# A streaming encoder layer on one core: 27 paired slots with all of conv a, weights summed by DMA, scan state kept in PSUM, branch A's norm moved into single slots

## The chip, the cores and the metric

The kernel is written for one Trainium2 chip and uses one of its cores. The metric is the device time of one execution in microseconds (us). The core has the engines TensorE (PE; the page shows its weight loads apart, as PEld), VectorE (DVE), ScalarE (ACT), GpSimd (POOL) and SyncE (SP), each with a queue of its own that it works off in order. Nearly all transfers are issued by SyncE; its queue and those of the other engines wait on semaphores. The program is written in Python with a tile library: pools hand out SBUF tiles by a tag with a fixed number of buffers, and a write into a tile waits until the last reader of the tile before it is done. PSUM has eight banks of 2 KB per partition.

## The reference

One layer over 1024 prompt rows and 32 sample rows (1056 columns in the kernel, which keeps channels on the partitions), with two branches from one input projection:

```python
proj = x @ w_in + b_in
a_val, a_glu, a_gate, z, xbc, dt_raw, g_a, g_b, g_p = jnp.split(proj, idx, axis=-1)

u = a_val * jax.nn.sigmoid(a_glu)
u, new_buf_a = causal_dwconv(u, buf_a, conv_a_w, conv_a_b)          # 31 taps
u = jax.nn.silu(layer_norm(u, norm_a_g, norm_a_b)) * jax.nn.silu(a_gate)
out_a = u @ w_a_out

xbc, new_buf_b = causal_dwconv(xbc, buf_b, conv_b_w, conv_b_b)      # 4 taps
xs, Bm, Cm = jnp.split(jax.nn.silu(xbc), [...], axis=-1)
dt = jax.nn.softplus(dt_raw + dt_bias)
y, h_new = ssd_scan(xs_h, dt, A, Bm, Cm, h0)       # chunks of 64 in the reference
y = (y + d_skip * xs_h).reshape(bsz, L, D_INNER)
out_b = gated_rmsnorm(y, z, gnorm_w) @ w_b_out

merged = sigmoid(g_a) * out_a + sigmoid(g_b) * out_b
x_new = layer_norm(ALPHA * x + merged @ w_out + sigmoid(g_p) * (p @ w_ple), ln_g, ln_b)
```

D_MODEL is 1024, the scan has 32 heads of 64 in 4 groups with a state of 128. In a scan chunk, with decays E and dec: y = (diagonal part) + E * (C times the carried state h), and h becomes dec * h + S, where S comes from the chunk's own B and x.

## The kernel before, in words

**Precision.** An fp32 product is made of three matmuls on parts of fewer bits: weights and activations are split into `hi` and `lo` (hi by ACT, lo = value - hi by DVE), and `three` (L191 ff.) issues hi*lo, lo*hi and hi*hi. So each 128-column tile of weights costs PE three passes and costs ACT and DVE a split.

**The stages in order.** The *start* loads x and p, splits weights (`wq_split`) and activations (`x_split`, `x_sum`, `t_split`), computes the embedding product p @ w_ple (`ple_group`, L569; eight tiles whose results are stored to `d_ple`) and dt (`dt_products`, `dt1`). Then come 24 *pair slots* P0 to P23 (`pair_slot`, L815): each makes two tiles of 128 projection columns with seven products of half size instead of eight (operands `OPND` with names like n2, t3, t4; weights r11, r12, r21, r22 and their sums), 168 matmuls of 264 columns in banks B0, B1, C and A. 40 *single slots* C0 to C39 follow (`slot`, L288): one tile each, 72 matmuls of 352 columns in three groups. B0 to B15 multiply by w_b_out, A0 to A7 by w_a_out, and W0 on by w_out with the last norm.

**The order of the work.** Each slot has named stages: loads first (`ld0`, the weights of slot s + 2, `ld`), stores (`st`), `d0`, the split of the next slot's weights, `a0`, `d1`, then the matmul groups with `a1` after the first third and `pm`, `a2` after the second, then `d2`, the fill, `pe` and `end`. `at(slot, stage, fn)` puts a piece of work into a stage; nothing else orders it, so what is written earlier stands earlier in each engine's queue. The fill (`run_fill`, L246) takes taps of conv a (31 DVE operations per half tile, `cae_u` and `cao_u`) until the DVE time that the program has counted for the slot reaches 11.0 us, or 14.2 us in a single slot with a scan chunk (in a pair: 2.82 us per position).

**Conv a and conv b.** Conv a needs pairs of tiles glu and val: five of the eight are made in pairs, tiles 5, 6 and 7 in single slots. Conv b (B, C and xs tiles) has three DVE taps per tile (`cb_t`) in the slot after it.

**Weights of a pair.** `pw_load` (L480) loads four quarters of 256 KB, `pw_sum` (L496) adds quarters on DVE into the tile `sx` or in place, and `pw_hi`, `pw_lo` split the seven results; `prep_act` and `prep_dve` (L503, L510) say at which of the seven positions of a pair this is done for the next.

**The scan.** `ssd_group` (L945) runs the 9 chunks (128 columns) of a group, one per single slot. In a chunk's first slot PE transposes (`pe_a`, at the end); in its second slot DVE and ACT prepare M, X and B2 (`prep`, stage `a0`), E is loaded, and PE makes `yd`, `yo` and S at the slot's end (`pe_d`, first in stage `pe`); in the third slot's `d0` DVE combines them (`update`, L1029): yo * E, + yd, four steps into the xs tiles, hT * dec, + S. The groups begin at C1, C10, C21 and C31.

**Branch A's norm.** Conv a's results are stored to `d_ca`. From C34 on (S_OB - 6 and later) they are loaded again, four at a time, summed (`ln_sum`), the sum over partitions is made on PE (`bcast_pe`, L328: three matmuls with ones onto all 128 rows) and broadcast through a row in memory (`ln_away`, `ln_back`); then the tiles are loaded again, centred and squared in B1 to B4, the reciprocal root follows (`rstd_chain`, L351), and `u_scale`, `u_act`, `u_mul` and the splits make w_a_out's operand. z tiles (`z_tile`, L1109) stay in SBUF until the scan of their group is done. Tiles for all of this are recycled in order by `tget` and `tput` (unit T), and smaller ones by U.

Of the kernel before, what the change touches and what calls it, by code (L numbers as in the profile page):

```python
# [60 lines left out]
def pair_tiles():  # L61

    gate = lambda n: ("gate", n, GATE_OFF[n // 8] + 128 * (n % 8))
    G = lambda n: (gate(n), gate(n + 1))
    C = lambda t: (("glu", t, O_GLU + 128 * t), ("val", t, O_VAL + 128 * t))
    X = lambda n: ("xs", n, O_X + 128 * n)
    return [G(0), G(2), C(0), G(8), G(4), G(10), G(6), C(1), G(12), G(16), G(14), C(2), G(18), G(20), G(22), G(24),
            C(3), G(26), G(28), G(30), C(4), (("B", 0, O_B), ("C", 0, O_C)), (X(0), X(1)), (X(2), X(3))]


def slot_tiles():
# [58 lines left out]
def emit(nc, tc, I, O, ctx):  # L130
# [197 lines left out]
    def bcast_pe(src, bks):  # L328

        out = []  # L330
        for (c0, c1), b in zip(GR, bks):
            ps = psum(b)
            mm(ps[:, :GN], ones, src[:, c0:c1])
            out.append(ps)
        return out

    def bcast_copy(pss, dst, scale=1.0):
        for (c0, c1), ps in zip(GR, pss):
            act(dst[:, c0:c1], ps[:, :GN], AF.Copy, scale=scale)
# [1446 lines left out]
```

## Time and profile before

| what | value |
|---|---|
| median of 3 runs | 1592.32 us (1592.23 to 1593.13) |
| the profiled execution | 1592.68 us, its span 1591.0 us |
| mean granted TensorE clock | 0.984 |
| busy: PE, DVE, ACT, POOL | 1527.2, 1296.9, 808.6, 3.0 us |
| start (up to P0) | 49.39 us |
| P0 to P23 | 49.39 to 558.78 |
| C0 to C39 | 558.78 to 1185.64 |
| B0 to B15 | 1185.64 to 1386.73 |
| A0 to A7, then W0 to the end | 1386.73 to 1481.12, then to 1591.0 |

How to read the lines below: a line of the timeline gives the start in us, the length in us, engine, line of the program, operation, output<-inputs, shapes and how many are put together. A line of the waits gives the waiting engine, what it makes and at which line, `<-` the engine and tile waited for, then the sum of the idle us, how many times, and the longest. A line of the groups ends with busy us, mean ns of one, and idle us before them. A line of the windows gives a stretch of the span, its length, the busy time of each engine with its instructions, the granted clock (PEclk), the DMA engines' share and GB/s. DMA lines give KB and the us from issue to landing.

### The profile page before, as it was taken

The numbers are of one execution on the slowest core, as the hardware profiler recorded it, in microseconds if no ns is written. First come the engines' busy times: TensorE is split into PE (matmuls) and PEld (weight loads), VectorE is DVE, ScalarE is ACT, GpSimd is POOL, SyncE is SP. The second block draws the span as 40 slices with busy tenths as digits, with TensorE's granted clock in tenths as the row PEclk, the third lists the DMA queues.
The fourth block names the chain that finished last, engine by engine and source line by source line (L and its number), as shares of the span: only waits on it lengthen the run. The fifth ranks groups of instructions, "written<-read, shape, count | busy, mean of one in ns | idle before, by whom it ended". The sixth has DMA issues, their size and how long they took to land.

```text
span 1591.0 us, 26642 instructions
## 1 busy us (share of the span) xinstructions
PE 1527.2 (96%) x10823; PEld 1481.8 (93%) x10823; DVE 1296.9 (82%) x1763; ACT 808.6 (51%) x1391; POOL 3.0 (0%) x14
## 2 busy tenths in 40 slices
PE   7899999999999989999999999999798999999997
PEld 6899999999999989999999999999688999999997
DVE  6888899999898599988988889888666887676654
ACT  6654334433434556666675666576564543333333
POOL 0000000000000000000000000000000000000000
PEclk9999999999999999999999999999899999999998
DMA  7252444442231134424252542336636171587422
GB/s 254 108 203 98 155 136 137 136 157 103 87 116 55 55 101 89 112 69 123 77 120 66 110 106 63 88 106 187 187 136 240 61 249 57 199 331 257 144 87 78
DMA packets 134377, 208.43 MB, mean 131 GB/s; under 512 B 28071, under 2 KB 84391, under 8 KB 134254
## 3 DMA queue, kind: packets, MB, share of 16 engines
q1 hardware_dynamic: 134254, 206.72, 41.9%
q8 instruction: 85, 1.39, 0.4%
q14 instruction: 38, 0.31, 0.1%
HBM read 156.49 MB, written 50.19 MB: 130 GB/s over the span
## 4 chain that ended last, share of the span: by engine, by line
PE 76%; DVE 12%; DMA 5%; ACT 4%; issue 2%; SPq 0%; DVEq 0%; ACTq 0%
PE ps L192 75%; DMA d_base<-cb_t 1%; PE ps L992 1%; DVE cao_u L176 1%; DVE cae_u L176 1%; DMA d_yn<-cbo_t 1%; DMA L_t<-d_accp 1%; DMA cat_t<-d_ca 1%; DVE sx L172 1%; DVE cb_t L176 0%; DVE wlo L172 0%; DMA d_gate<-ga_t 0%; DVE dt_u L176 0%; DVE acc_t L172 0%; DVE cb_u L176 0%
## 5 line engine op out<-in xcount | busy, mean ns | idle before, releaser
L176 DVE SCALAR_TENSOR_TENSOR cae_u<-uin_u,par,cae_u 128x1086 f32<-128x1086 f32 x120 | 161.3, 1344 | 0.0
L176 DVE SCALAR_TENSOR_TENSOR cao_u<-uin_u,par,cao_u 128x1086 f32<-128x1086 f32 x112 | 150.5, 1344 | 0.0
L186 ACT ACTIVATE whi<-wraw 128x1024 fp32r<-128x1024 f32 x65 | 68.5, 1054 | 67.5 <-PE ps L192 42.8
L186 ACT ACT_TABLE_LOAD x77 | 98.8, 1283 | 7.1 <-DMA out_conv_b<-vin_t 4.9
L172 DVE TENSOR_TENSOR wlo<-wraw,whi 128x1024 fp32r<-128x1024 f32 x65 | 79.3, 1219 | 24.6 <-ACT whi L186 24.5
L186 ACT ACTIVATE vin_t<-ps,par 128x352 f32<-128x352 f32 (+5 forms) x88 | 39.1, 476 | 107.3 <-PE ps L192 107.3
L186 ACT ACTIVATE L_t<-L_t,tk 128x128 f32<-128x128 f32 (+1 forms) x272 | 80.4, 381 | 0.0
L176 DVE SCALAR_TENSOR_TENSOR cb_t<-vin_t,par,cb_t 128x1059 f32<-128x1059 f32 x60 | 79.1, 1319 | 1.2
L186 ACT ACTIVATE zt_t<-ps,par 128x352 f32<-128x352 f32 x48 | 26.4, 554 | 75.3 <-PE ps L192 75.0
L172 DVE TENSOR_TENSOR acc_t<-acc_t,ps 128x352 f32<-128x352 f32 x72 | 36.6, 518 | 33.1 <-PE ps L192 33.0
L186 ACT ACTIVATE gb_t<-ps,par 128x528 f32<-128x528 f32 x26 | 18.2, 701 | 88.7 <-PE ps L192 74.8
L172 DVE TENSOR_TENSOR M<-ps,E 128x512 f32<-128x512 f32 (+1 forms) x32 | 20.4, 637 | 49.0 <-PE ps L192 45.3
L192 PE MATMUL ps<-n2l,w_2h 128*128 128x264 f32 x192 | 55.5, 289 | 3.7 <-ACT ga_t L186 3.7
L192 PE MATMUL ps<-t3l,w_4h 128*128 128x264 f32 x192 | 54.6, 284 | 2.3 <-ACT ga_t L186 2.3
L192 PE MATMUL ps<-n2h,w_2l 128*128 128x264 f32 x192 | 55.2, 288 | 0.0
L192 PE MATMUL ps<-n2h,w_2h 128*128 128x264 f32 x192 | 55.1, 287 | 0.0
L192 PE MATMUL ps<-t4l,w_6h 128*128 128x264 f32 x192 | 54.6, 285 | 0.3 <-ACT gb_t L186 0.3
L192 PE MATMUL ps<-t3h,w_4l 128*128 128x264 f32 x192 | 54.5, 284 | 0.0
L192 PE MATMUL ps<-t4h,w_6h 128*128 128x264 f32 x192 | 54.4, 284 | 0.0
L192 PE MATMUL ps<-t4h,w_6l 128*128 128x264 f32 x192 | 54.4, 283 | 0.0
L192 PE MATMUL ps<-t3h,w_4h 128*128 128x264 f32 x192 | 54.3, 283 | 0.0
L192 PE MATMUL ps<-x0l_t,whi 128*128 128x352 f32 x117 | 41.9, 358 | 8.9 <-ACT sg_t L186 5.0
(878 smaller groups left out, 5910.4 us busy)
## 6 DMA issues: line engine op xcount, KB each, us to landing
r<-in_w SPq DMA_DIRECT2D x96, 256.0 KB, 3.1
wraw<-in_w SPq DMA_DIRECT2D x39, 512.0 KB, 4.3
L_t<-d_accp SPq DMA_DIRECT2D x30, 512.0 KB, 6.5
d_yn<-cbo_t SPq DMA_DIRECT2D x16, 528.0 KB, 3.6
wraw<-in_wb SPq DMA_DIRECT2D x16, 512.0 KB, 3.6
yraw_t<-d_yn SPq DMA_DIRECT2D x15, 528.0 KB, 7.7
gs_t<-d_gate SPq DMA_DIRECT2D x15, 528.0 KB, 5.9
E<-d_expa SPq DMA_DIRECT2D x56, 128.0 KB, 4.7
```

Of the source, the lines that this page charges most:

```text
L172: nc.vector.tensor_tensor(out, a, b, op)
L176: nc.vector.scalar_tensor_tensor(out, a, s, b, op0, op1)
L186: nc.scalar.activation(out, a, f, **kw)
L192: nc.tensor.matmul(out, l, r, start=start, stop=stop, skip_group_check=more)
L992: nc.tensor.transpose(pX[:nt, j * P:(j + 1) * P], XS[j][:, sl], ident)
```

## The change

Six things are changed together.

1. **27 pairs, 34 singles.** The glu and val tiles 5 to 7 go into three more pairs; a conv a pair stands in every third place of the table instead of more widely apart.

```diff
-    return [G(0), G(2), C(0), G(8), G(4), G(10), G(6), C(1), G(12), G(16), G(14), C(2), G(18), G(20), G(22), G(24),
+    return [G(0), G(2), C(0), G(8), G(4), C(1), G(10), G(6), C(2), G(12), G(16), C(3), G(14), G(18), C(4), G(20), G(22), C(5),
...
-    return ca(5) + bcx(1) + z(0) + ca(6) + bcx(2) + z(1)[:2] + ca(7) + bcx(3) + z(1)[2:] + z(2) + z(3)
+    return bcx(1) + z(0) + bcx(2) + z(1) + bcx(3) + z(2) + z(3)
...
-    SSD0 = [S_CL + i for i in (1, 10, 21, 31)]
+    SSD0 = [S_CL + i for i in (1, 10, 19, 28)]
```

2. **Weights of a pair.** `pw_sum` is gone. The sums s1, s3 and s2 are made in memory transfers: SyncE loads the first summand and GpSimd issues DMAs that add the others onto it, one for s1 and s3 and two for s2; r12, the third that s2 takes, is added later (`pw_s4`). That is six loads by SyncE (four before) and five DMAs by GpSimd (none before).

```diff
+    PARTS = {"r11": ("11",), "r12": ("12",), "r22": ("22",), "s1": ("21", "22"), "s3": ("21", "11"), "s2": ("11", "21", "22")}
...
     def pw_load(i, n):
         if i < len(PAIRS):
-            t = raw_tile(n, f"{n}_{i}")
-            load(t, I["w1"][2 * i + (n[1] == "2"), :, 512 * (n[2] == "2"):512 * (n[2] == "2") + 512])
-            pr[i, n] = t
+            t = pr[i, n] = raw_tile(n, f"{n}_{i}")
+            load(t, pw_src(i, PARTS[n][0]))
+            for q in PARTS[n][1:]:
+                nc.gpsimd.dma_start(t, pw_src(i, q), accum_op=ALU.add)
+
+    def pw_s4(i):
+
+        if i < len(PAIRS):
+            nc.gpsimd.dma_start(pr[i, "s2"], pw_src(i, "12"), accum_op=ALU.add)
```

On DVE, in a pair (names w_1l to w_4l are lo halves of the seven weights, r and s the quarters and sums, ga, gb and sg results, cae and cao taps), the order before is:

```order
L172 TENSOR_TENSOR w_1l<-sx_2595,w_1h 128x512
L172 TENSOR_TENSOR sx_2595<-r_9_2421,r_9_2423 128x512
L172 TENSOR_TENSOR ga_t_2555<-ga_t_2555,ps_2663 128x528
L172 TENSOR_TENSOR gb_t_2556<-gb_t_2556 128x528
L172 TENSOR_TENSOR w_2l<-sx_2595,w_2h 128x512
L172 TENSOR_TENSOR w_3l<-r_9_2522,w_3h 128x512
L172 TENSOR_TENSOR sx_2595<-r_9_2522,sx_2595 128x512
L172 TENSOR_TENSOR ga_t_2555<-ga_t_2555,ps_2597 128x528
L172 TENSOR_TENSOR w_4l<-r_9_2421,w_4h 128x512
```

The same place after the change, still on DVE:

```order
L171 TENSOR_TENSOR w_1l<-s_9_2505,w_1h 128x512
L175 SCALAR_TENSOR_TENSOR cae_u_2324<-uin_u_1867,par,cae_u_2324 128x1086
L175 SCALAR_TENSOR_TENSOR cao_u_2356<-uin_u_1867,par,cao_u_2356 128x1086
L171 TENSOR_TENSOR sg_t_2605<-sg_t_2605,ps_2720 128x528
L171 TENSOR_TENSOR w_2l<-s_9_2441,w_2h 128x512
L175 SCALAR_TENSOR_TENSOR cae_u_2324<-uin_u_1867,par,cae_u_2324 128x1086
```

The two sums into sx are gone, and taps of conv a stand between the splits.

3. **The start.** `wq_split(2)` and `(3)` stand in the work list ahead of the sums T3 and N2, the embedding's results 0 to 5 and 7 go to tiles of xpool (tags n2l, t3l, t3h) instead of U, `dt1` goes into the work list, and P0's weights come by `pw_load` as in 2.

4. **The scan.** The matmuls of the carried part (`pe_o`) go to stage `pm`, after two thirds of the slot; DVE's `carry` (stage `d2`) writes hT * dec into the bank of S and multiplies y by E in PSUM; `pe_d` adds onto both banks; `update` is a copy of S by ACT and the four steps into xs.

```diff
-                yd, S = psum(5), psum(7)
+                y, S = d["y"], d["S"]
...
-                    mm(yd[64 * u:64 * u + 64, j * P:j * P + nt], X[:nt, 64 * h:64 * h + 64], d["L3"][:, h, :])
...
-                mm(S, B2[:nt, :], M[:nt, :512])
...
+                    mm(y[64 * u:64 * u + 64, j * P:j * P + nt], X[:nt, 64 * h:64 * h + 64], d["L3"][:, h, :],
+                       i == 0 and j == 0, True, True)
+                mm(S, B2[:nt, :], M[:nt, :512], i == 0, True, True)
...
+            def pe_o(i=i, sl=sl, nt=nt):
+
+                d = st[i]
+                d["y"], d["S"] = psum(6), psum(7)
+                if i:
+                    for j in range(4):
+                        mm(d["y"][:, j * P:j * P + nt], hcols(i)[:, j * P:(j + 1) * P], Ct_[0][:, sl], j == 0, True, True)
+
+            def carry(i=i, nt=nt):
+                if i:
+                    d = st[i]
+                    h3 = hcols(i).rearrange("p (h c) -> p h c", h=8)
+                    tt(d["S"][:, :].rearrange("p (h c) -> p h c", h=8), h3,
+                       decb[:, 8 * g:8 * g + 8, i].unsqueeze(2).to_broadcast([P, 8, 64]), ALU.mult)
+                    y3 = v4(d["y"][:, :])[:, :, :nt]
+                    tt(y3, y3, v4(d["E"][:, :4 * nt]), ALU.mult)
...
+                act(hc, S)
...
+            at(s0 + i + 1, "pm", pe_o)
+            at(s0 + i + 1, "d2", carry)
```

On PE, at the end of a slot with a chunk (cbo tiles are xs, B and C after conv b, hT the state, L the decays, x7 the last operand of the slot's matmuls), before:

```order
L192 MATMUL ps_7176<-x7h_t_118,whi_6944 128x352
L192 MATMUL ps_7208<-L_t_6927,X_3_7106 64x128 x8
L192 MATMUL ps_7218<-cbo_t_6158,hT_t_6505 128x128 x4
L192 MATMUL ps_7209<-M_3_7105,B_3_7107 128x512
L992 MATMUL ps_7224<-ident,cbo_t_6401 128x128
```

After, first at two thirds of such a slot, then at its end:

```order
L191 MATMUL ps_8033<-x7h_t_117,whi_7837 128x352
L191 MATMUL ps_8059<-cbo_t_7040,hT_t_7392 128x128 x4
L191 MATMUL ps_8074<-x0l_t_104,whi_7837 128x352
...
L191 MATMUL ps_8074<-x7h_t_117,whi_7837 128x352
L191 MATMUL ps_8059<-L_t_7823,X_3_7998 64x128 x8
L191 MATMUL ps_8060<-M_3_7997,B_3_7999 128x512
L966 MATMUL ps_8120<-ident,cbo_t_7287 128x128
```

The four matmuls on hT have moved ahead of the last third, and the eight on L now add onto the same tile (ps_8059) that DVE multiplies between the two. On DVE the slot after, with `update` and `prep`, reads before:

```order
L172 TENSOR_TENSOR M_4_7259<-ps_7374,E_4_7239 128x512
L172 TENSOR_TENSOR M_4_7259<-M_4_7259,ps_7364 128x512
L176 SCALAR_TENSOR_TENSOR cbo_t_6401<-cbo_t_6401,par,M_4_7259 128x128
...
L172 TENSOR_TENSOR hT_t_6505<-hT_t_6505,decb 128x512
L172 TENSOR_TENSOR hT_t_6505<-hT_t_6505,ps_7365 128x512
L172 TENSOR_TENSOR wlo_7412<-wraw_7237,whi_7410 128x1024
L172 TENSOR_TENSOR M_5_7417<-ps_7380,tk 128x512
```

After, from the last step into xs to the first tap of conv b (the two rows that write ps are `carry`):

```order
L175 SCALAR_TENSOR_TENSOR cbo_t_7402<-cbo_t_7402,par,ps_8059 128x128
L171 TENSOR_TENSOR wlo_8147<-wraw_7978,whi_8145 128x1024
L171 TENSOR_TENSOR M_4_8152<-ps_8120,tk 128x512
L171 TENSOR_TENSOR X_4_8153<-ps_8120,tk 128x512
L171 TENSOR_TENSOR M_4_8152<-ps_8121,mask 128x128
L171 TENSOR_TENSOR L_t_7976<-L_t_7976,M_4_8152 128x1024
L171 TENSOR_TENSOR ps_8215<-hT_t_7392,decb 128x512
L171 TENSOR_TENSOR ps_8214<-ps_8214,E_4_8133 128x512
L175 SCALAR_TENSOR_TENSOR cb_t_8160<-vin_t_7973,par,cb_t_8160 128x1059
```

The four operations of 512 columns at the slot's head are gone, and two stand behind `prep`, ahead of the taps.

5. **Branch A's norm.** Its base A0 is S_OB - 17, in the single slots: the sums in C17 and C18, the mean's matmuls after C18, and from C21 to C28 one tile per slot is loaded, centred, squared and stored again (`ca_away`); the u steps go one tile per slot from B6 on. A z tile that is made more than four slots ahead of its use is stored to `d_z` and loaded again (five tiles).

```diff
-        at(B + t // 4 * 2, "ld", ca_load, t)
-        at(B + 1 + t // 4 * 2, "d1", ln_center, t)
...
+    A0 = B - 17
...
+        c = A0 + 4 + t
+        at(c - 1, "ld", ca_load, t)
+        at(c, "d1", ln_center, t)
+        at(c, "a1", ln_square, t)
+        at(c + 1, "st", ca_away, t)
```

6. **Sums over partitions.** `rows_pe` takes the place of `bcast_pe` and of the sums in hi and lo parts: three matmuls with 32 columns of ones into three groups of 32 partitions of one bank.

```diff
+    def rows_pe(src):
+
+        ps = psum(5)
+        for g, (c0, c1) in enumerate(GR):
+            mm(ps[32 * g:32 * g + 32, :GN], ones[:, :32], src[:, c0:c1])
+        return ps
```

More of the change, by code (lines that the diff above doesn't have):

```diff
@@ L206, in emit @@
     nc.gpsimd.memset(ones, 1.0)
-    nc.gpsimd.memset(ones_r[:, :].bitcast(F32), 1.0)
     nc.gpsimd.memset(epsb, EPS)
@@ L225, in emit @@
     d_yn = dpool.tile([16, P, NT], F32, name="d_yn")
+    d_z = dpool.tile([16, P, NT], F32, name="d_z")
     d_ca = dpool.tile([8, P, NT], F32, name="d_ca")
@@ L325, in slot, with rows_copy @@
         run(s, "end")
[L328 to L339, printed above, removed]
+    def rows_pe(src):
[3 more added lines that the diff above has]
+        return ps
+    def rows_copy(ps, dst, scale=1.0):
+        for g, (c0, c1) in enumerate(GR):
+            act(dst[0:1, c0:c1], ps[32 * g:32 * g + 1, :GN], AF.Copy, scale=scale)
     def newton(r, m, t):
@@ L461, in emit @@
     r_quad(0, 1)
-    w0 = xpool.tile([P, 8, H], F32, tag="t3l", name="w0", bufs=1)
+    w0 = ppw.tile([P, 8, H], F32, tag="o0h", name="w0", bufs=1)
     wdt = xpool.tile([P, 1024], F32R, tag="t3h", name="wdt", bufs=1)
@@ L575, in ple_group @@
             three(ps[:, :GN], wh[:, w], wl[:, w], ph[:, k, c0:c1], pl_[:, k, c0:c1], k == 0, k == 1)
-        if g == 0 and m in (4, 6):
-            both = xpool.tile([P, 2, NT], F32, tag=f"t3{'hl'[m // 2 - 2]}", name=f"pl{m}", bufs=1)
+        if g == 0 and m in (0, 2, 4, 7):
+            both = xpool.tile([P, 2, NT], F32, tag={0: "n2l", 2: "t3l", 4: "t3h", 7: "t3l"}[m], name=f"pl{m}", bufs=1)
             pls[m], pls[m + 1] = both[:, 0, :], both[:, 1, :]
-        if g == 0 and m < 4:
+        if g == 0 and m == 6:
             pls[m] = U.get([P, NT], F32, "pl")
@@ L743, in step @@
             f(*a)
-    for n in ("r11", "r21", "r22", "r12"):
+    for n in ("r11", "s1", "s2", "r12", "s3"):
         pw_load(0, n)
@@ L753, in emit @@
     xs2 = lambda n: [(x_sum, n, q) for q in range(2)]
-    work.extend(xs4("B11") + xs4("B12") + xs2("D1") + [(wdt_split,)] + xs4("B21") + xs4("B22") + xs2("T3") + xs2("N2"))
+    ts2 = lambda n, q: [(t_split, n, q, i) for i in range(2)]
+    work.extend(xs4("B11") + xs4("B12") + xs2("D1") + [(wdt_split,)] + xs4("B21") + xs4("B22") + [(wq_split, 2), (wq_split, 3)])
     for m in range(4):
@@ L781, in emit @@
     x_put((1, 1))
-    for n in ("r21", "r22"):
-        pw_load(1, n)
     pw_hi(0, 3, "r12")
     pw_lo(0, 3, "r12")
+    pw_load(1, "r12")
     for q in range(2):
@@ L1109, in z_tile, with away, back @@
     def z_tile(g, j, zt, s):
-        q = {}
+        q = {"z": zt}
+        def away():
+            load(d_z[4 * g + j], zt)
+            tput(zt)
+        def back():
+            q["z"] = tget(name="zt")
+            load(q["z"], d_z[4 * g + j])
+        if s - cur[0] > 4:
+            at(cur[0] + 1, "st", away)
+            at(s - 1, "ld", back)
         def gate():
             x = XSs[4 * g + j]
-            tt(x, x, zt, ALU.mult)
+            tt(x, x, q["z"], ALU.mult)
         def square():
-            act(zt, XSs[4 * g + j], AF.Square)
+            act(q["z"], XSs[4 * g + j], AF.Square)
         def add():
             if j == 0:
-                zst[g] = zt
+                zst[g] = q["z"]
             else:
-                tt(zst[g], zst[g], zt, ALU.add)
-                tput(zt)
+                tt(zst[g], zst[g], q["z"], ALU.add)
+                tput(q["z"])
         at(s, "d1", gate)
```

163 lines of the change are left out of this document (60 added, 103 removed).

## The prediction, made before the changed kernel was run

> **What bounds the kernel now.** I read the page first, then the busy time by stage, then who TensorE (PE) waits for, stage by stage. The page:
>
> ```profile
> span 1591.0 us, 26642 instructions
> ...
> PE 1527.2 (96%) x10823; PEld 1481.8 (93%) x10823; DVE 1296.9 (82%) x1763; ACT 808.6 (51%) x1391; POOL 3.0 (0%) x14
> ...
> PEclk9999999999999999999999999999899999999998
> ...
> PE 76%; DVE 12%; DMA 5%; ACT 4%; issue 2%; SPq 0%; DVEq 0%; ACTq 0%
> ```
>
> PE is busy for 96% and most of the chain that ended last is PE. So two things can shorten the run: less PE work, and fewer stretches in which PE waits or runs at half clock. The table by stage says where those are (its rows are: the start; P0 to P6; P7 to P22; P23 to C1; C2 to C35; C36 to B3):
>
> ```profile
> core 0: us, PE busy (x) PEld busy (x) DVE busy (x) ACT busy (x) POOL busy (x), PEclk, DMA share, GB/s
> 0.00:49.39 49.39, 36.99 (x193) 35.45 (x193) 34.74 (x55) 33.14 (x69) 1.93 (x12) 0.93 0.63 232
> 49.39:206.40 157.01, 147.11 (x1186) 145.63 (x1186) 135.58 (x182) 73.92 (x130) 1.09 (x2) 0.99 0.39 136
> 206.40:533.07 326.67, 326.67 (x2691) 326.67 (x2689) 294.28 (x374) 130.44 (x222) 0.00 (x0) 1.00 0.34 115
> 533.07:591.08 58.01, 49.49 (x327) 48.33 (x326) 44.79 (x52) 33.77 (x56) 0.00 (x0) 0.94 0.32 88
> 591.08:1105.36 514.28, 513.70 (x3455) 483.35 (x3453) 456.07 (x609) 332.44 (x608) 0.00 (x0) 0.99 0.40 98
> 1105.36:1245.58 140.22, 121.23 (x750) 112.71 (x748) 98.03 (x127) 75.11 (x125) 0.00 (x0) 0.94 0.54 179
> ```
>
> ```profile
> 908.07:1000.39 92.32, 92.32 (x633) 86.80 (x632) 80.97 (x114) 58.91 (x112) 0.00 (x0) 1.00 0.33 79
> 1386.73:1467.84 81.11, 81.11 (x507) 81.11 (x505) 59.24 (x83) 31.14 (x41) 0.00 (x0) 1.00 0.82 296
> 728.70:732.10 3.40, 3.40 (x14) 3.40 (x14) 3.37 (x8) 1.03 (x2) 0.00 (x0) 0.50 0.42 90
> ```
>
> Undisturbed stretches give PE's price of each kind of slot: P7 to P22 is 326.67 / 16 = 20.42 us per pair; C23 to C28, each with one scan chunk, 92.32 / 6 = 15.39 us; A0 to A6, plain single slots, 81.11 / 7 = 11.59 us. A chunk therefore costs 3.80 us. What a stage took beyond these prices is loss. P0 to P6 took 157.01 against 7 x 20.42 + 0.9 (nine transposes) = 143.8: 13.2 lost. The start has 49.39 - 36.99 = 12.4 idle and about 3.5 at 0.93 of the clock: 16 lost. P23 to C1 lost about 12 (8.5 idle, the rest clock). C36 to B3 is 4 x 15.39 + 14.49 + 3 x 11.59 and some 2.7 of sums over partitions, 113.6; it took 140.22: 26.6 lost. PE's waits name the culprits:
>
> ```profile
> PE ps L192 <- ACT acc_t L186: 6.9, 4, 4.4
> PE ps L192 <- DVE M L172: 6.9, 1, 6.9
> PE ps L192 <- ACT ga_t L186: 6.0, 2, 3.7
> PE ps L192 <- DVE t4l L172: 5.8, 2, 5.4
> PE ps L192 <- ACT sg_t L186: 5.0, 1, 5.0
> PE ps L192 <- ACT zt_t L186: 4.8, 2, 3.9
> PE ps L192 <- DVE wq2l L172: 4.4, 1, 4.4
> PE ps L192 <- DVE vin_t L172: 3.5, 1, 3.5
> ```
>
> **Pairs for singles.** Six single slots (conv a tiles 5 to 7) become three pairs: 6 x 11.59 - 3 x 20.42 = 69.54 - 61.26 = 8.3 us less PE work. It is on the path, since PE never idles in either undisturbed stretch.
>
> **Weights summed by DMA.** This takes four DVE additions out of each pair and puts five GpSimd DMAs and two SyncE loads in.
>
> ```profile
> L172 DVE TENSOR_TENSOR sx<-r,r 128x512 f32<-128x512 f32 x48 | 33.2, 692 | 1.7
> ...
> r<-in_w SPq DMA_DIRECT2D x96, 256.0 KB, 3.1
> ```
>
> 4 x 0.69 = 2.8 us per pair leave DVE. From P7 on that brings PE nothing: DVE already has 20.42 - 294.28 / 16 = 2.0 us to spare per pair, and the fill puts conv a taps of the three added tiles in the room. It does shorten DVE's queue in P0 to P2, before the fill. The added traffic is 7 x 256 KB per 20.42 us, 90 GB/s on top of 115; by the stage's share of 0.34 that makes about 0.6, so I let it hide. No trace shows a DMA that adds: the nearest row is the plain load, 3.1 us to landing. The tightest of the five is the fourth summand of s2: its issue follows position 4 (14.6 us into the pair) and ScalarE (ACT) wants it at position 0 of the next pair (23.3), so 8.7 us for one landing; I take cost 0 and treat a slow one as a rival. The Trainium skill ("DMA: Bandwidth & Descriptors", section "Anatomy of one DMA — SWDGE (gpsimd) path") gives about 2.0 us and the bytes at 436 GB/s for a GpSimd DMA, which would be an estimated 2.6 us here and would leave the sum as it is; no run here shows one yet.
>
> **The start.** Weight splits 2 and 3 now stand ahead of the sums T3 and N2, the embedding's results go to xpool tiles instead of recycled units, and the last sum for P0 no longer stands in ACT's queue.
>
> ```profile
> ACT pl_u L186 <- PE ps L192: 6.0, 1, 6.0
> DVE x7l_t L172 <- ACT x7h_t L186: 5.0, 1, 5.0
> ...
> ACT w_5h L186 <- DVE sx L172: 2.8, 1, 2.8
> ...
> DVE t3l L172 <- DMA d_ple<-pl: 2.4, 1, 2.4
> ```
>
> PE's matmuls that pl_u reads were long done, so I read the 6.0 as a wait for a recycled unit whose store had not landed; DVE stood behind it for 5.0. Gone should be the 4.4 on wq2l with its 3.5 of half clock, some 1.4 around the dt products, about 2 of the 3.7 on ga_t (ACT sat 2.8 behind sx), and about 3 in P1 to P3, where DVE is 2.8 ahead per pair: 14 of the 29 lost in these two stages. Bounds: 5 (the store wait stays) and 20. The wait on d_ple for t3l stays.
>
> **Branch A's norm.** Its sums, centring and squares leave C36 to B5 for C17 to C28, one tile per slot, at the price of eight more 528 KB stores and five z tiles sent away and back.
>
> ```profile
> ACT lnS_t L186 <- DMA d_yn<-cbo_t: 16.1, 1, 16.1
> ```
>
> That row is the head of today's worst chain: lnS takes over a tile whose store is queued behind the tile loads, the DVE sums wait for ACT, and PE stands 6.9 us before the mean. In the new place lnS inherits a tile that only ACT read last. I take 22.6 of the 26.6 back and leave 4 for new short waits; bounds 8 and 26.6. B0 to B2 now carry chunks, which only moves PE work.
>
> **Scan state in PSUM.** The four matmuls of y's carried part move from the slot's end to two thirds of the slot, and DVE's two products (`carry`) come between them and the rest, so PE gains a wait at each slot's end. Behind it on DVE stand the conv b taps and the fill; PE waits for it with pe_d.
>
> ```profile
> 652.14 0.68 DVE L172 TENSOR_TENSOR M<-ps,E 128x512 f32<-128x512 f32 x1
> ...
> 659.75 4.03 DVE L176 SCALAR_TENSOR_TENSOR cb_t<-vin_t,par,cb_t 128x1059 f32<-128x1059 f32 x3
> ```
>
> ```profile
> L172 DVE TENSOR_TENSOR hT_t<-hT_t,decb 128x512 f32<-128x512 f32 x24 | 16.4, 685 | 0.0
> ```
>
> From a chunk's update to its taps DVE needs 659.75 - 652.14 = 7.6 us, of which the four operations of 0.69 leave or move: 4.9 stay ahead of carry. The update can start when PE ends pe_d, some 1.5 us before the slot; so DVE is ready near 3.4 us (to 6 with branch A's tasks), PE offers the product at 7.7 + 1.0 = 8.7, and needs carry by 12.7. Carry takes 1.4: 2.6 us of room. DVE's whole load, 80.97 / 6 = 13.5 us, stays under 15.39, and two of its four 0.69 us operations go. PE's count of matmuls is unchanged. Cost 0.
>
> **Sums over partitions.** Seven times three fp32 matmuls onto 32 columns each take the place of two full ones of this kind and five in hi/lo parts.
>
> ```profile
> 617.40 1.10 PE L192 MATMUL ps<-L_t,X 128*64 128x128 f32 x16
> 618.42 1.16 PE L192 MATMUL ps<-cbo_t,hT_t 128*128 128x128 f32 x8
> 619.42 1.02 PE L192 MATMUL ps<-M,B 128*128 128x512 f32 x2
> ```
>
> ```profile
> 588.62 1.94 PE L192 MATMUL ps<-cbS_t,ones 128*128 128x352 f32 x6
> 590.39 0.60 PE L992 MATMUL ps<-ident,cbo_t 128*128 128x128 f32 x4
> ```
>
> ```profile
> 783.30 0.32 PE L192 MATMUL ps<-vl_t,ones_r 128*128 128x352 f32 x1
> ...
> 784.26 0.32 PE L192 MATMUL ps<-x0l_t,whi 128*128 128x352 f32 x1
> ```
>
> Before: 2 x 1.77 + 5 x 0.96 = 8.3 us. The 16 half-width matmuls take 1.02 us, as long as 8 full ones: halves run two at a time. With two at a time the new form is 0.88 us, 7 x 0.88 = 6.2: 2.2 less. Bounds: all three at once 0.59 (4.2 less), one after another 1.77 (4.1 more). The Trainium skill ("TensorE: Matmul & The Clock Gate", section "Part 3: Packing small matmuls — row/col tiling") has three 32-column tiles at 2.38 times the speed of one after another; by that a sum would be 0.74 us and the total 0.9 us lower.
>
> **What stays.** The last three pairs (B and C, then xs) and C0 and C1 keep their order, and so their 12 us. The row at 728.70 shows 3.4 us at clock 0.50 with PE never idle before it, another such stretch stands at 868.7; I keep both. The same page of the Trainium skill (section "Part 1: The HAM clock gate (the "warmup" mystery)") ties the half clock to a window of about 3.4 us without activity; by that these two would not exist and the total would be 3.4 us lower, and the trace speaks against it here.
>
> **The sum.** 1592.68 (the profiled execution: its span 1591.0 and 1.7 around it) - 8.3 - 14 - 22.6 - 2.2 = 1545.6. The median is 0.36 below that execution: 1545.2, say 1545.
>
> **The rivals.** First, DVE comes late to carry. For: the fill holds DVE near 15 us in the slots before C13, and ACT's copy of S is a new link. Against: 2.6 us of room and DVE's 1.9 idle per slot. It decides from 2.6 us of lateness; each us more costs 32 chunks x 1 = 32 us: 1577 at one us.
>
> Second, branch A's stall moves instead of going. C16 and C17 again load four 528 KB tiles each, ahead of the E that carry needs on SyncE's queue, with as few free tiles as C36 has. The waits on M and zt_t (6.9 + 4.8) and their clock come back, some 16 us: 1561.
>
> Third, and on the other side: the summed weights come late. If a summing DMA takes d to land, s2 is late beyond 8.7 us; ACT and DVE then stand at position 0, and DVE has 2.0 to give. From d = 10.7 each pair grows: (d - 10.7) x 25. At d = 12.6, four times the plain 3.1, the 47 us are eaten; at 13, slower: 1603. For: every such DMA also reads its destination, POOL issues them in order behind waits for loads. Against: the engines' share is a third.
>
> Fourth, everything works: all 26.6 and 20 come back and sums run three at once, 47 + 4 + 6 + 2 = 59 off: 1533.
>
> **How the numbers follow.** Forecast 0.62, carry late 0.12, stall moved 0.11, sums late 0.07, all of it 0.08. The range 1531 to 1578 takes in the first, second and fourth rival and the bounds of start, norm and sums; it leaves out the third and small tails. A measurement of this kernel tells about 0.2% (3.2 us) from no change. Only the third rival reaches that side: faster 0.91, same 0.02, slower 0.07.
>
> **What would show it.** After: span near 1544; pairs still 20.4 us; 34 single slots at 15.4 with a chunk; no 16 us wait on lnS; P0 ending near 64 instead of 75.9; waits on a new pair of rows (carry's ps) under 5 us; GpSimd's DMAs landing in 3 to 6 us; sums over partitions at 0.6 to 0.9 us. Wrong it is if pairs grow beyond 20.6, if chunk slots grow, or if C16 to C28 show waits over 4 us in sum.

## The result: 8% slower, and the profile after

Four runs of the changed kernel took 1720.72 to 1733.02 us, median 1723.43; four of the kernel before 1591.66 to 1593.13, median 1592.28. The ratio is 1.083 (95% interval 1.079 to 1.088). Forecast were 1545 in a range of 1531 to 1578. The profiled execution has a span of 1719.1 us, 128.1 more than before.

The page of the changed kernel, the lines that answer to those of before:

```profile
span 1719.1 us, 27206 instructions
...
PE 1554.3 (90%) x10895; PEld 1496.0 (87%) x10895; DVE 1197.4 (70%) x1628; ACT 828.3 (48%) x1436; POOL 121.1 (7%) x148
...
PE 41%; DMA 21%; DVE 16%; issue 9%; ACT 7%; SPq 3%; POOL 2%; DVEq 0%; POOLq 0%; ACTq 0%
...
s<-in_w POOLq DMA_DIRECT2D x135, 256.0 KB, 5.4
```

DVE has 100 us less to do, as planned, and PE is busy for 90% instead of 96%: the chain that ended last is now PE for 41% (76% before), with transfers at 21%. The adding DMAs land 5.4 us after their issue, where the nearest row of before gave 3.1 for a plain load.

The table by stage, first of the changed kernel (the start; P0 to P26; C0 to B15; A0 to A7):

```profile
0.00:44.42 44.42, 34.93 (x192) 34.58 (x193) 33.15 (x52) 33.36 (x69) 5.41 (x15) 0.96 0.88 297
44.42:707.30 662.88, 586.88 (x4547) 578.83 (x4546) 491.94 (x598) 242.72 (x422) 115.66 (x133) 0.96 0.66 170
707.30:1510.36 803.06, 739.17 (x4800) 691.55 (x4799) 542.63 (x750) 477.07 (x819) 0.00 (x0) 0.96 0.47 135
1510.36:1609.72 99.36, 95.40 (x578) 94.87 (x577) 70.90 (x98) 37.06 (x48) 0.00 (x0) 0.97 0.75 270
```

And of the kernel before, the same stages (P0 to P23; C0 to B15 with six more singles):

```profile
0.00:49.39 49.39, 36.99 (x193) 35.45 (x193) 34.74 (x55) 33.14 (x69) 1.93 (x12) 0.93 0.63 232
49.39:558.78 509.39, 495.96 (x4042) 494.30 (x4042) 444.16 (x577) 218.56 (x376) 1.09 (x2) 0.99 0.35 118
558.78:1386.73 827.95, 803.38 (x5232) 763.26 (x5231) 688.20 (x904) 481.68 (x821) 0.00 (x0) 0.98 0.43 120
1386.73:1481.12 94.39, 92.96 (x578) 92.67 (x577) 70.24 (x98) 37.08 (x48) 0.00 (x0) 1.00 0.77 276
```

With three pairs at 20.42 put in for six singles at 11.59, the 128 us are made up of: the start -5.0; the pairs 662.9 - (509.4 + 61.3) = +92.2; C0 to B15 803.1 - (828.0 - 69.5) = +44.6; A0 to A7 +5.0; the end -0.5; the exchange itself -8.3. So there are two losses to explain. A pair takes 24.5 us on average, where the 24 pairs of before took 21.2 and the undisturbed ones among them 20.4. And in the single slots, where about 25 us were to be won, 45 are lost.

**The pairs.** GpSimd's queue and ACT's in P10 to P12 of the changed kernel (P11 starts on PE at 325.92), with the wait in square brackets:

```profile
318.42 0.82 SPq L188 DMA_DIRECT2D r<-in_w  x2
319.33 3.61 SPq L188 DMA_DIRECT2D s<-in_w  x2
```

```profile
325.43 0.86 POOL L468 DMA_DIRECT2D s<-in_w  x1 [9.99 <-DVE cae_u L175]
329.50 2.15 POOL L468 DMA_DIRECT2D s<-in_w  x2 [3.21 <-DMA s<-in_w]
330.77 1.75 POOL L473 DMA_DIRECT2D s<-in_w  x1
```

```profile
342.52 0.63 ACT L185 ACTIVATE w_5h<-s 128x512 fp32r<-128x512 f32 x1 [12.73 <-DMA s<-in_w]
```

```profile
336.88 1.26 DVE L175 SCALAR_TENSOR_TENSOR ga_t<-bt_u,ga_t 128x1056 f32<-128x1056 f32 x1 [4.93 <-DMA bt_u<-in_xT]
...
344.40 0.69 DVE L171 TENSOR_TENSOR w_0l<-r,w_0h 128x512 fp32r<-128x512 f32 x1
```

```profile
345.11 1.03 SPq L188 DMA_DIRECT2D r<-in_w  x2
```

The reader sees a ring. The load of r11 for the pair after next waits on SyncE for DVE's w_0l; the load of s2 stands behind it (319.33). GpSimd adds r21 to it at 325.43, when it has landed (the profile puts this wait down to `cae_u`, whose tile the transfer does not touch), and r22 only when r21 has landed, at 329.50. The fourth summand for the *next* pair (L473) stands in the queue behind these: issued at 330.77, although position 4 of P10 (which began at 303.57) would have ended near 318 at PE's price. It lands 11.7 us later among the 512 and 528 KB transfers of that moment, ACT's w_5h waits 12.73 us for it, DVE's w_5l, w_6l and w_0l follow, and behind w_0l (344.40) the next loads go out at 345.11: the ring begins again 26.7 us after the 318.42, where PE needs 20.6.

P11 holds a second wait as well: DVE stands 4.93 us for the load of x (bt_u), so this slot alone does not tell the two apart; e2 and e13 below do. Over P7 to P22 the fourth summand goes out 3.3 us after DVE's w_2l, the last reader of its tile, and lands 8.0 us after its issue, on average.

**The single slots.** From C2 to C32 of the changed kernel PE waits six times for the carried part, and once besides, in C2; ACT's longest single waits in the same stretch are for stores:

```profile
PE ps L191 <- DVE ps L171: 44.8, 6, 10.7
PE ps L191 <- DVE L_t L171: 3.5, 1, 3.5
```

```profile
ACT L185 <- DMA d_yn<-cbo_t: 22.2, 2, 12.8
ACT L185 <- DMA d_ca<-cat_t: 19.4, 2, 10.2
ACT L185 <- DMA out_conv_b<-vin_t: 12.4, 1, 12.4
...
ACT cb_t L185 <- DMA out_conv_b<-vin_t: 11.6, 1, 11.6
```

One of the six, in C12 (891.1 to 915.5), on SyncE, ACT and DVE:

```profile
893.65 1.35 SPq L188 DMA_DIRECT2D d_yn<-cbo_t  x2
```

```profile
902.02 1.28 ACT L185 ACT_TABLE_LOAD   x1 [9.36 <-DMA d_yn<-cbo_t]
...
904.40 0.26 ACT L185 ACTIVATE B<-ps 128x128 f32<-128x128 f32 x1
```

```profile
904.69 0.29 DVE L171 TENSOR_TENSOR M<-ps,mask 128x128 f32<-128x128 f32 x1 [9.57 <-ACT B L185]
...
910.27 0.69 DVE L171 TENSOR_TENSOR ps<-ps,E 128x512 f32<-128x512 f32 x1
```

The silu of conv b takes over a tile whose store to d_yn was issued in this very slot; ACT stands 9.36 us until it has landed; B, M and `carry` stand behind it, and PE waits 7.1 us. With a slower clock behind the wait (0.86 granted on average over the slot, 1.00 in the next), C12 takes 24.4 us instead of 15.3; C16, C22, C24, C25 and C26 take 23.5 to 28.6 in the same way (in C24 DVE stands at the norm's root, which ACT makes late).

A seventh wait stands just behind this stretch, in C33, which takes 27.5 us; there ACT waits for the store of a z tile, one of the new stores of part 5 of the change:

```profile
PE ps L191 <- DVE ps L171: 9.9, 1, 9.9
```

```profile
ACT y2h_t L185 <- DMA d_z<-zt_t: 12.6, 1, 12.6
```

### The profile page after: what moved, and what is told of

The parts are those of the page before. It is cut to its first block, busy times and chain, and to the rows that moved or that the text cites. A ratio compares the mean times of both kernels' runs of the same rounds, so it can differ in the third digit from the quotient of the medians.

```text
span 1719.1 us, 27206 instructions
## 1 busy us (share of the span) xinstructions
PE 1554.3 (90%) x10895; PEld 1496.0 (87%) x10895; DVE 1197.4 (70%) x1628; ACT 828.3 (48%) x1436; POOL 121.1 (7%) x148
## 3 DMA queue, kind: packets, MB, share of 16 engines
q0 software_dynamic: 19440, 35.40, 12.4%
## 4 chain that ended last, share of the span: by engine, by line
PE 41%; DMA 21%; DVE 16%; issue 9%; ACT 7%; SPq 3%; POOL 2%; DVEq 0%; POOLq 0%; ACTq 0%
PE ps L191 40%; DMA s<-in_w 12%; DVE cae_u L175 3%; SPq L188 2%; DVE cao_u L175 2%; POOL s L468 2%; DMA d_ca<-cat_t 2%; DMA d_base<-cb_t 2%; DVE cb_t L175 1%; DMA d_yn<-cbo_t 1%; DMA out_conv_b<-vin_t 1%; DVE w_0l L171 1%; PE ps L966 1%; DMA d_gate<-ga_t 1%; DVE w_6l L171 1%
## 5 line engine op out<-in xcount | busy, mean ns | idle before, releaser
L468 POOL DMA_DIRECT2D s<-in_w x108 | 94.0, 931 | 548.2 <-DMA s<-in_w 355.2
L185 ACT ACT_TABLE_LOAD x77 | 98.8, 1283 | 56.1 <-DMA d_yn<-cbo_t 22.2
L191 PE MATMUL ps<-t3l,w_4h 128*128 128x264 f32 x216 | 66.1, 306 | 24.3 <-ACT sg_t L185 13.5
L191 PE MATMUL ps<-L_t,X 128*64 128x128 f32 (+1 forms) x528 | 39.6, 299 | 51.0 <-DVE ps L171 47.5
L185 ACT ACTIVATE w_5h<-s 128x512 fp32r<-128x512 f32 x27 | 17.0, 630 | 136.2 <-DMA s<-in_w 136.2
L171 DVE TENSOR_TENSOR w_5l<-s,w_5h 128x512 fp32r<-128x512 f32 x27 | 18.7, 691 | 91.6 <-ACT w_5h L185 91.4
L191 PEld LDWEIGHTS ps<-L_t,X 128*64 128x64 f32 (+1 forms) x528 | 31.2, 152 | 58.7 <-DVE ps L171 49.9
L175 DVE SCALAR_TENSOR_TENSOR cbo_t<-cbo_t,par,ps 128x128 f32<-128x128 f32 (+1 forms) x144 | 38.7, 331 | 47.4 <-PE ps L191 47.4
L191 PEld LDWEIGHTS ps<-t3l,w_4h 128*128 128x128 f32 x216 | 43.7, 203 | 26.8 <-ACT sg_t L185 14.1
L191 PE MATMUL ps<-t3h,w_4l 128*128 128x264 f32 x216 | 64.7, 300 | 0.0
L191 PE MATMUL ps<-t3h,w_4h 128*128 128x264 f32 x216 | 64.5, 299 | 0.0
```

Source lines behind the costliest of these rows:

```text
L171: nc.vector.tensor_tensor(out, a, b, op)
L175: nc.vector.scalar_tensor_tensor(out, a, s, b, op0, op1)
L185: nc.scalar.activation(out, a, f, **kw)
L191: nc.tensor.matmul(out, l, r, start=start, stop=stop, skip_group_check=more)
L468: nc.gpsimd.dma_start(t, pw_src(i, q), accum_op=ALU.add)
```

## The experiments

Theory 1: the pairs are long because the summed weights come late through the ring above. Theory 2: the single slots are long because ACT waits for recycled tiles behind stores. The rivals are named in the expectations. Times of single runs stand beside one of the kernel before on the same chip (from e13 on, the median of seven). In the diffs, minus is the changed kernel, or the run that the text names.

### e1: sums on DVE again

```diff
-            for q in PARTS[n][1:]:
-                nc.gpsimd.dma_start(t, pw_src(i, q), accum_op=ALU.add)
...
+            tt(pr[i, dst], pr[i, a], pr[i, b], ALU.add)
```

SyncE's loads are four per pair again, in the places of before.

> The changed kernel with the four additions per pair back on DVE (as before the change) and no GpSimd DMA; the conv a taps keep their places, so DVE gets 2.8 us more per pair. Theory 1 (the pairs' loss is the weights that come late through the adding DMAs): the waits of ACT for s vanish, and a pair costs what DVE then needs, 18.5 + 2.8 = 21.3 us (PE's own price is 20.4): 27 pairs in 575 instead of 663 us, the whole near 1636. Rival (the conv a pairs at every third place, or the new start, make the pairs long): pairs stay near 24.5 us and the whole above 1700. The single slots keep their long waits under both.

Measured: 1661.49 us (before: 1598.46). The pairs took 599.6 us, 63 less, and ACT's waits for s are gone; the single slots kept theirs. Theory 1 holds against its rival, but a pair is 22.2 us on average, not 21.3: from P17 on they took 20.7 to 21.5, as worked out, but P5, P6, P9, P12 and P15 took 22 to 27. Something else is in there (below).

### e2: the fourth summand first on GpSimd's queue

```diff
-            pw_load(i + 2, "s2")
+            pw_load(i + 2, "s2", True)
...
             pw_s4(i + 1)
+            pw_add(i + 2, "s2")
+            pw_add(i + 2, "s1")
```

> Only the order on GpSimd's queue differs from the changed kernel: the fourth summand of s2 for the next pair is issued ahead of the adds of s2 and s1 of the pair after that; the number and size of the transfers is the same. Theory 1a (a loop: the fourth summand stands in the queue behind adds that wait for loads, these loads wait for DVE's w_0l, and DVE waits for the fourth summand): the loop is cut, 8.7 us are there for a landing of 5.4 to 10 us, pairs fall to 20.4 to 21.5 us, the whole to 1625 to 1650. Theory 1b (adding DMAs are too slow, or the traffic is): pairs stay above 23.5 us, the whole above 1690.

Measured: 1670.12 us (before: 1598.46); pairs in 605.9 us, 57 less, and P17 to P25 at 20.6 us each. Over all 135 adding DMAs the median landing is 6.0 us, no faster. But the one that is waited for has changed in two ways: from P7 to P22 the fourth summand goes out 0.4 us after w_2l instead of 3.3, and being first in its group it lands in 3.7 us instead of 8.0. Its row here, with the wait for w_2l in the brackets:

```profile
307.79 0.86 POOL L478 DMA_DIRECT2D s<-in_w  x1 [12.19 <-DVE w_2l L171]
```

ACT's longest wait has gone from w_5h to w_1h, where it harms less:

```profile
ACT w_1h L185 <- DMA s<-in_w: 53.7, 18, 7.2
DVE w_5l L171 <- ACT w_5h L185: 17.7, 7, 4.8
```

The same rows of the changed kernel, P7 to P22:

```profile
ACT w_5h L185 <- DMA s<-in_w: 99.9, 16, 12.7
DVE w_5l L171 <- ACT w_5h L185: 63.5, 13, 7.5
```

So the order on the queue, with the same transfers, makes nearly the whole difference: theory 1a. The order sets when the awaited transfer goes out (2.9 us sooner) and also how soon it lands (4.3 us less). The total stayed above its 1650, for the loss in P2 to P15 stayed.

### e3: no adding

```diff
-                nc.gpsimd.dma_start(t, pw_src(i, q), accum_op=ALU.add)
+                nc.gpsimd.dma_start(t, pw_src(i, q))
...
```

> The same DMAs from GpSimd without the adding: each overwrites its tile, so the weights s1, s2 and s3 are not sums. Theory 1a (order and waits on the queue set the pair): pairs stay within 0.7 us of 24.5, the whole between 1700 and 1730. Theory 1b in its form that adding is what takes long (the destination is read too): landings fall clearly below 5.4 us and pairs below 22 us, the whole under 1660.

Measured: 1669.13 us (before: 1598.46); pairs in 607.8 us, 22.5 each; landings at 3.4 us instead of 5.4:

```profile
q0 software_dynamic: 10800, 35.40, 6.5%
...
s<-in_w POOLq DMA_DIRECT2D x135, 256.0 KB, 3.4
```

Theory 1a's number missed. The ring can explain it: two landings of adds stand in it, and from P7 to P22 r21's onto s2 took 3.1 us instead of 3.8 and the fourth summand's 4.8 instead of 8.0. These 3.9 us less would bring the 23.9 us of these pairs to 20.0, below PE's 20.6; that is worked out from the landings, not tested by itself. So the time of the adds and the order on the queue are both needed for the loss: with either one mended (e2, e3) the late pairs are back at 20.6.

### e4: prep first in its stage

```diff
-            at(s0 + i + 1, "a0", prep)
+            todo[(s0 + i + 1, "a0")].insert(0, (prep, ()))
```

> The changed kernel with the scan's prep put first in its stage a0, so that ACT's copy of B and DVE's M stand ahead of conv b's silu. Theory 2 (in the single slots ACT waits with the silu or the first tap for a recycled tile whose store was issued in the same slot, 9 to 13 us; B, M, the carried part and so PE stand behind it): PE's waits for the carried part in C12, C16, C22, C25 and C26 (35 us, with the slow clock after them 48) vanish, the one of C24 (9.8) stays because there DVE is held by the root of the norm: 1723 - 48 = 1675. Rival 2b (DVE is late for the carried part of itself, through the conv b taps and the fill): the waits stay, 1720.

Measured: 1741.97 us (before: 1598.46); PE's waits in C12, C16, C22, C25 and C26 stayed. The order shows that the edit did nothing there: the silu is put in front later, with the same insertion. In C12 to C26 it is the changed kernel run again and decides nothing. It took 21 us more than the profiled run of that kernel, some 10 of them in the pairs and C0 to C33, where next to nothing moved: single runs can differ by that much.

### e5: the scan as before

```diff
-            at(s0 + i + 1, "pm", pe_o)
-            at(s0 + i + 1, "d2", carry)
```

> The changed kernel with the scan as before the change (yo at the slot's end, all of y and the state put together in update); the fill keeps its places. Theory 2 (ACT's wait for a recycled tile is the cause, the scan's form only sets how much DVE work stands between that and PE): PE then waits for L and M alone, which DVE has 1.2 to 5.0 us earlier than the carried part in C12, C16, C22, C25 and C26, and in C24 prep is done before DVE stands at the norm's root: the six waits fall from 44.8 to about 16 us, and with the slow clock after them some 35 us go, 1688. Rival 2b (the carried part in PSUM is itself the cost): all 44.8 and their clock go, about 65 us, 1658.

Measured: 1718.38 us (before: 1591.96), 5 less than the changed kernel's median. PE's waits only changed their names (C2 to C32):

```profile
PE ps L191 <- DVE L_t L171: 24.5, 5, 7.5
PE ps L191 <- ACT zt_t L185: 9.7, 2, 6.9
PE ps L191 <- DVE L_u L171: 4.9, 1, 4.9
```

Both numbers missed: 35 and 65 were to go. But rival 2b falls: without `carry`, the same ACT waits reach PE by way of L and of zt.

### e6: prep in d0

```diff
-            at(s0 + i + 1, "a0", prep)
+            at(s0 + i + 1, "d0", prep)
```

> The changed kernel with the scan's prep moved ahead of the weight split and of conv b's silu (stage d0, behind update), which the run before this one did not do, since the silu is put in front again. Theory 2: ACT copies B before it comes to the silu that waits for a recycled tile, so DVE has M and the carried part in time; the waits of PE in C12, C16, C22, C25 and C26 (35 us, 48 with the clock) vanish, C24 keeps its 9.8: 1675. If ACT's wait is not what holds the chain, they stay: above 1715.

Measured: 1706.36 us (before: 1591.96). Of the 35 us of waits in C12, C16, C22, C25 and C26 1.8 are left, as theory 2 says; but C13, C17, C23 and C27, the slots behind, now have 13, and C24 went from 9.8 to 16.0. ACT loses its 9 to 13 us in this order too; they come out one slot later.

### e7: the tile that has been free longest

```diff
...
-        return (T if T.free else U).get(list(shape), dtype, name)
+        since = lambda u: PUT.get(u.free[0][1], 0) if u.free else 999
+        pool = U if since(U) < since(T) and S_CL + 2 <= NOW[0] < S_OA or not T.free else T
+        return pool.get(list(shape), dtype, name)
```

> No instruction of the changed kernel moves; from C2 on a tile is taken from whichever of the two recycled sets has the one that was given back longest ago, so that in C2 to B3 a tile given back in the same slot behind a store is taken once instead of 19 times. Theory 2: ACT's waits for d_yn, d_ca and out_conv_b of 9 to 13 us go, and with them PE's six waits of 44.8 us and their slow clock, about 60 us: 1663. Rival 2b: the waits for the carried part stay, above 1715.

Measured: 1646.33 us (before: 1591.96). PE's waits from C2 to C32:

```profile
PE ps L198 <- DVE ps L178: 3.8, 3, 2.3
PE ps L198 <- DVE L_t L178: 1.9, 1, 1.9
PE ps L198 <- DVE cbo_t L182: 0.5, 1, 0.5
```

One wait of ACT for a store is left in this stretch, in C17, the one tile that is still taken in the slot in which it was given back:

```profile
ACT cbo_u L192 <- DMA out_conv_b<-vin_u: 6.0, 1, 6.0
```

C12, C22, C25 and C26 are back at 15.3 us, and C33 is at 16.5. C0 to B15 takes 736.0 us, 67 less, and A0 to A7 92.9 instead of 99.4. No instruction moved, only the memory under the tiles: theory 2 is shown.

### e8: both together

The edits of e2 and e7.

> The fourth summand issued first (as in the run with that order) and the longest free tile taken, together. If the two causes stand side by side, the gains add: 55 in the pairs and 60 in the single slots off 1723, 1608; if the pairs' lateness only moves into the single slots, less than 80 are gained, above 1643.

Measured: 1592.94 us (before: 1591.96), pairs 605.6, C0 to B15 738.0: the gains add, and the changed kernel is back where the one before stands.

### e9: two of the sums on DVE

On top of e7; s1 and s3 stay adding DMAs.

```diff
-    PARTS = {"r11": ("11",), "r12": ("12",), "r22": ("22",), "s1": ("21", "22"), "s3": ("21", "11"), "s2": ("11", "21", "22")}
+    PARTS = {"r11": ("11",), "r12": ("12",), "r22": ("22",), "s1": ("21", "22"), "s3": ("21", "11")}
...
+            pw_sum(i + 1, "s1", "r11")
...
+            pw_sum(i + 1, "s2", "r12")
```

> On top of the run with the longest free tile: s1 and s3 stay with one adding DMA each, s2 and its fourth summand are made by two DVE additions again (s1 + r11, then + r12), so that no adding DMA is wanted sooner than 15 us after its issue. Theory 1: pairs from P7 on cost PE's price of 20.6 us, since DVE's 18.5 + 1.4 stays below it (412 us for the 20, 480 in the changed kernel), and some 15 us stay lost in P0 to P6: 1565 to 1575. Rival (the pairs' loss comes as much from the traffic as from the order): pairs stay above 22 us, 1595 or more.

Measured: 1595.26 us (before: 1594.61). The pairs took 607.5, no better than e2: P16 to P25 were at 20.6, P2 to P15 again lost some 40 us, half of it in P2 to P6. There the rival's number came out, with no adding DMA awaited. DVE's waits in P7 to P16 say what it is:

```profile
DVE ga_t L182 <- DMA bt_u<-in_xT: 15.3, 3, 6.1
DVE w_5l L178 <- ACT w_5h L192: 10.9, 3, 4.0
```

The base tiles' load of x is issued in the slot in which DVE adds it, and with a conv a pair in every third place these slots are now those of the conv a pairs too (P5, P8, P11, P14).

### e10: the kernel before with e7's rule

The edit of e7 in the kernel before, from C20 on.

> The kernel before the change with the rule of the longest free tile, from C20 on. If tiles given back behind a store also make the stall of C36 to B3 there (16.1 us on lnS), 10 to 17 of its 26.6 us go: 1575 to 1582. If that stall has another cause, 1590 to 1593.

Measured: 1581.37 us (before: 1594.61): 13.2 less. No wait on lnS is left; the recycled tile was the cause of that wait, and of about half of the 26.6 us. C37 still takes 24.6 us instead of 27.9.

### e11: e9 with the scan as before

The edit of e5 in e9.

> The run e9 with the scan as before the change, the fill in its places. Without ACT's waits the carried part is in time (theory 2), so the two forms agree within 4 us. If the form in PSUM costs something of its own, this run is faster by over 5 us; if it gains what it saves on DVE, slower by over 5.

Measured: 1610.79 us, 15.5 more than e9. With tiles in time, the scan in PSUM is a gain, against "within 4 us". C14, C18, C23, C29 and C32 are longer in e11, by PE's waits for ACT and L, and B0 to B15 by 6.2 us; which part of the old form does it was not tried.

### e13 and e17: the base tiles moved

```diff
-    return [G(0), G(2), C(0), G(8), G(4), C(1), G(10), G(6), C(2), G(12), G(16), C(3), G(14), G(18), C(4), G(20), G(22), C(5),
+    return [G(0), G(2), C(0), G(4), G(8), C(1), G(6), G(10), C(2), G(16), G(12), C(3), G(18), G(14), C(4), G(20), G(22), C(5),
...
-        at(s + 2, "d1", add)
+        at(s + 2, "a1", add)
```

> On top of e9: the gate pairs that start a base tile stand one place later, so that the base's additions no longer fall into a conv a pair, and they run after the third product instead of the first, so that the load of x, which is issued in the same slot, has 8 us more to land. If what is still lost in P2 to P16 of e8 and e9 (37 us) is DVE's wait for that load on top of conv a's work, P5, P8, P9, P11, P12, P14 and P15 fall to 20.6 to 21.5 us and some 20 go: near 1575. If it is the traffic or the weights, the pairs after a conv a pair stay at 25: above 1590.

Measured: 1570.38 us (before: 1592.64 median); P7 to P25 took 20.6 to 21.6 us each. P2, P3 and P5 still took 24.7, 28.8 and 23.8; what holds them was not tried. e17 has the first hunk alone:

> e13 without the later additions: only the places of the gate pairs that start a base tile are moved. If the pairs P8 to P15 were long because the base's additions fell into a conv a pair, they stay at 20.6 to 21.5 us as in e13 and the whole is within 5 us of it; if DVE's wait for the load of x in the same slot is what counted, P6, P9, P12 and P15, which now hold the additions, take 23 us or more and 10 to 15 us come back.

Measured: 1583.01 us (before: 1591.82 median). P6, P9, P10, P12, P13, P15 and P16 took 22.2 to 24.3, and DVE waited 11.9 us for x in P7 to P16, in e13 not at all. So, by one run each, the place brings some 10 of the gain over e9 and the moment some 13.

### e14 and e15: prep too; all sums on DVE

e14 is e13 with the edit of e6, e15 is e13 with the edit of e1.

> e13 with the scan's prep ahead of conv b's silu as well: the one tile that is still given back and taken in the same slot (C17, 4.5 us with the clock) then costs nothing, the rest stays: 3 to 6 us less than e13. If prep's new place holds ACT or DVE up elsewhere, no gain or a loss.

> e13 with all four additions per pair on DVE and no adding DMA. DVE then needs 21.3 us per pair against PE's 20.6 while conv a is filled in, 0.7 x 20 = 14 more; without adding DMAs the pairs P2 to P6, which have no fill or little, may get up to 10 back: within 10 us of e13. If it is faster than e13, DMA summing has no use here at all.

Measured: e14 1573.18 us, ratio to before 0.988 (0.987 to 0.990); e15 1577.07, 0.990 (0.989 to 0.992). Prep's new place gains nothing. Sums on DVE cost 7 us against e13, less than the 14 worked out, since P2 to P6 are faster with them.

### e16: e13 in rounds

> The same kernel as e13, timed in five rounds: 0.986 of the kernel before, within 0.4%.

Measured: 1569.27 us, ratio 0.986 (0.984 to 0.988): the version that beats both. Against the change it makes two of the four sums on DVE, takes the longest free tile, and moves the base tiles. Of its 22.6 us, 13.2 come to the kernel before as well by e7's rule alone (e10, one run); the change itself, so mended, is then worth some 9, against the 47 forecast.

## Why the prediction was wrong, point by point

- **Weights summed by DMA** is the step that failed in the pairs: "8.7 us for one landing; I take cost 0". It took the issue of the fourth summand for the end of position 4, 14.6 us into the pair. Its tile is free only behind w_2l, which even in the undisturbed pairs of e2 (P17 to P22) ends at 17 us, so that the room was nearer 6 us than 8.7. And the queue that it stands in was not walked through: the adds of s2 and s1 for the pair after that are ahead of it, the first of these waits for a load that waits for DVE's w_0l, and w_0l waits for the fourth summand. From P7 to P22 it was issued 27.2 us into the pair on average, 12.6 later than taken, and landed 8.0 us after that. Much of the 12.6 is the ring's own work, for w_2l ended at 23.9 instead of 17. The third rival had the right place ("POOL issues them in order behind waits for loads") but priced only the landing, and by its formula 8.0 us would have been no loss. e2 gets 57 us back by the order alone, e1 63.
- **Branch A's norm and the second rival.** A stall of the second rival's kind happened, and the rival was too small: it came not as one of 16 us for want of free tiles at C16 alone but as seven in C12 to C33, and PE paid for them with most of the 67 us that e7 gets back. The step "in the new place lnS inherits a tile that only ACT read last" looked at one tile of the recycled set. With 34 singles for the same conv b, z and scan tiles, 19 tiles from C12 to C33 are given back behind a store and taken in the same slot, and in seven slots PE waits. Whether the fewer slots or the new stores of d_ca and d_z make them was not tried apart. With e7's rule C0 to B15 takes 736.0 us against 828.0 - 69.5 = 758.5 before, 22.4 less, where 22.6 for the norm and 2.2 for the sums were forecast. That these agree is luck: with the same rule the kernel before needs 812.4 there (e10), and 812.4 - 69.5 = 742.9 leaves 6.9 for the change, in which the sums have 3.3 and the new form of the scan a larger part (e11). No run moves the norm alone, so whether its move gains anything stays open.
- **Scan state in PSUM.** Cost 0, with 2.6 us of room, was right: in e7 PE waits 3.8 us in all for it from C2 to C32. That the form gains (e11) was not forecast. The first rival is refuted as a cause of its own (e5, e7); in the changed kernel `carry` only passes ACT's wait on.
- **Pairs for singles.** The price of a pair without waits is 20.57 us in all versions of the change, against 20.42 in the profile of before: some 4 of the 8.3 us. The kernel before has 20.57 too in e10's run, so that is not the change.
- **"The fill puts conv a taps in the room"** held from P17 on. In P2 to P15 some 40 us are lost that no term had (e9). In P7 to P15 the conv a pairs in every third place meet the base tiles, and DVE has no room for a wait of 4 to 6 us there; moving them (e13) brings 23 us back. Of the rest some 16 us lie in P2, P3 and P5, and their cause is open.
- **The start.** 5 of the 14 came. PE starts P0 at 44.42 instead of 49.39, but the waits around the dt products and in P0 only changed names (5.3 for t4l, 4.2 for pl), and P0 to P3 took 92 us in e1 as before. The expected end of P0 at 64 was 70.0.
- **Sums over partitions.** Mis-sized to the good. The row of the changed kernel, with the one that follows on PE:

```profile
733.14 0.79 PE L191 MATMUL ps<-cbS_t,ones 128*32 128x352 f32 x6
733.86 0.66 PE L966 MATMUL ps<-ident,cbo_t 128*128 128x128 f32 x4
```

  A sum takes 0.72 us (0.88 was taken): 7 x 0.72 = 5.0 instead of 8.3, 3.3 less. That is 2.46 times as fast as the 1.77 of before; the Trainium skill's 2.38 for three 32-column tiles ("TensorE: Matmul & The Clock Gate", section "Part 3: Packing small matmuls — row/col tiling") agrees, and its 0.74 was nearer than my row.

The chance of 0.07 for the slow side came from a single landing time. What was left out were the two places where a wait feeds itself or is handed on: a ring through the queues of SyncE, GpSimd, ACT and DVE, and a set of tiles worked off in order.

## What to carry to other kernels

Before work is moved onto a queue that works in order, walk the queue entry by entry: what stands ahead, what that waits for, and whether the wait leads back to the entry itself; here the length of that ring, not the time of one transfer, set the period, and a transfer issued behind others also landed later. When a change packs the same tiles into fewer slots, list each tile that is given back behind a store and taken in the same slot; taking the longest free one moves no instruction and was worth 77 us here and 13 in the kernel before. A transfer issued in the slot that uses it is hidden only as long as that slot has room.

## What the runs showed of the hardware

An adding DMA from GpSimd landed in 5.4 us at the median, the same transfer without adding in 3.4; it was cut into 19440 packets instead of 10800 for the same 35.40 MB and took 12.4% of the DMA engines' span instead of 6.5%. The row of the changed kernel beside that of e3:

```profile
q0 software_dynamic: 19440, 35.40, 12.4%
```

For a GpSimd DMA of this size the figures of the Trainium skill ("DMA: Bandwidth & Descriptors", section "Anatomy of one DMA — SWDGE (gpsimd) path") come to an estimated 2.6 us; both measured medians are longer, and beside transfers of 512 and 528 KB one took 11.7. In this kernel DVE writes a bank of PSUM that PE then accumulates onto, and at 0.69 us the write takes as long as the same product into SBUF did before (685 ns, in the prediction's row of hT_t):

```profile
L171 DVE TENSOR_TENSOR ps<-hT_u,decb 128x512 f32<-128x512 f32 x24 | 16.6, 690 | 0.0
```
